# A hybrid diffusion block on one core: gate and up projections by seven products a pair, and the hidden split moved into the down stage

## The chip, the cores and the metric

The kernel runs on one core of a Trainium2 chip. The metric is device microseconds of one execution, the median over several runs. The profiled execution gives the span from its first to its last instruction. Engines are named as in the profile: PE (TensorE), PEld (its weight loads), DVE (VectorE), ACT (ScalarE), POOL (GpSimd), SP (the queue that issues DMAs).

## What is computed

One transformer-like layer over 512 latent tokens of width 1024 (with a context of 256 tokens): a token mixer of three branches (a state-space scan, a convolution, a pooling mixer), merged by gates and projected, and then a dense SwiGLU with a hidden width of 2816:

```python
def swiglu(h, w_gate, w_up, w_down):
    return (jax.nn.silu(h @ w_gate) * (h @ w_up)) @ w_down
...
        h_lat = modulate(rms_norm(x, norm2_g[l]), mod_lat[3], mod_lat[4])
        x = x + mod_lat[5] * swiglu(h_lat, ffn_w_gate[l], ffn_w_up[l], ffn_w_down[l])
...
    return rms_norm(x, final_g)
```

The change touches `swiglu` alone: 512 x 1024 times 1024 x 2816 twice, and 512 x 2816 times 2816 x 1024.

## The kernel before

Tokens lie along the free dimension (512 columns), features along the 128 partitions. Each projection is tiled by 128 output features. A weight tile of a unit is 128 x 1024: eight blocks of 128 x 128, one for each 128 input features. Operands are F32R, and each product is made in three passes: a number is split into a high part, rounded to F32R, and a low part, the rest. `mm3` (lines 131 to 136) adds hi·hi, hi·lo and lo·hi into one PSUM bank, so a unit with eight input tiles is 24 matmuls of 512 columns.

`load_unit` (115 to 125) loads a weight tile from SP into one of three `wr` tiles (line 112), casts it on ACT to `whi` (line 120) and subtracts on DVE to `wlo` (line 122 or 124); `whi` and `wlo` have three tiles each. `split` (127 to 129) does the same to any tile. PSUM has three banks "mm" and four "ps".

Up to line 1064 the token mixer and the residual run; they end with `h2`, the eight normalised input tiles as hi and lo (`hh`, `hl`), made by halves of the tokens (1047 to 1054). Then:

- Lines 1072 to 1080: the first three units, by halves of the tokens (256 columns), so that they can start before the second half of `h2` is there.
- Lines 1083 to 1102: the units u = 3 to 43; an even u is the gate, an odd one the up part of pair u // 2, 22 pairs in all. The gate's bank goes through Silu on ACT (1091), the up bank is multiplied with it on DVE (1093), and the product is split at once into `fh` and `fl` (1095). In eight of the pairs an `ada` step (line 900, DVE) makes a column of the last modulation vector from a 512 KB load of `wada`.
- Lines 1105 to 1122: eight down tiles of 66 matmuls, with three weight units each, the residual, and the final norm; the last tile goes by halves.

Engines run their queues in order. Since line 1016's `load_unit` all this is issued through `nc.vector`, `nc.scalar` and `nc.tensor`, and the tile framework orders each queue by a planner's priorities; `tc.high_priority` moves a step forward. A step waits for what it reads, and for the readers of what its tile held before.

## Time and profile before

| what | value |
|---|---|
| median of 3 runs | 1000.64 us (1000.06 to 1000.73) |
| span of the profiled execution | 998.8 us |
| time of the profiled execution beside it | not listed; the median is 1.8 us above the span |
| PE, DVE, ACT busy | 977.7, 670.9, 411.9 us |
| gate and up units u = 3 to 43 | 641.20 to 866.40 us |
| down tiles | 866.40 to 988.9 us |

A matmul's busy time runs from its start to a modelled end and overlaps the next; the pace of PE is read from starts or from counts in a stretch. A row's "idle before" is the time in which its engine stood still just ahead of it, with what ended it.

### The profile page before, as it was taken

What the parts mean: (1) busy time and instruction counts of PE and PEld (TensorE: products, weight loads), DVE (VectorE), ACT (ScalarE), POOL (GpSimd) and SP (SyncE); (2) the same over time, 40 slices, a digit from 0 to 9 for tenths busy, and PEclk for the clock granted to TensorE, in tenths of its full rate; (3) what the DMA queues carried; (4) which work ended last, traced back from release to release, by engine and by line L of the source; (5) the groups of instructions that cost most, each with busy time, mean ns of one, the idle gap of its engine ahead of it and who ended that gap; (6) DMA issues with size and microseconds to landing.
All of it is one profiled execution on the core that took longest, in us unless ns stands there. A gap on an engine that the chain in (4) does not pass through costs nothing.

```text
span 998.8 us, 12631 instructions
## 1 busy us (share of the span) xinstructions
PE 977.7 (98%) x4820; PEld 789.1 (79%) x4820; DVE 670.9 (67%) x1014; ACT 411.9 (41%) x598; POOL 20.7 (2%) x68
## 2 busy tenths in 40 slices
PE   6999999999999999999999999999999999999996
PEld 4678888888887776676787889988888888888885
DVE  5589999978889999999877846734453333332333
ACT  5683643244454233346655545523223232232331
POOL 0100000000000000001000000000000000000000
PEclk9999999999999999999999999999999999999998
DMA  9653334322122466545689851433443222233312
GB/s 364 264 181 106 121 112 145 107 85 78 43 85 77 135 203 201 188 152 170 193 278 326 320 184 43 149 106 126 148 141 133 91 99 94 85 100 95 96 58 85
DMA packets 59149, 144.04 MB, mean 144 GB/s; under 512 B 11728, under 2 KB 22608, under 8 KB 57936
## 3 DMA queue, kind: packets, MB, share of 16 engines
q1 hardware_dynamic: 59088, 143.23, 43.0%
q8 instruction: 38, 0.62, 0.2%
q14 instruction: 23, 0.19, 0.1%
HBM read 126.44 MB, written 16.78 MB: 143 GB/s over the span
## 4 chain that ended last, share of the span: by engine, by line
PE 89%; DVE 4%; DMA 4%; ACT 1%; issue 1%; SPq 0%; DVEq 0%; ACTq 0%
PE mm L134 26%; PE mm L136 26%; PE mm L135 25%; DMA wr<-in_wso_dram 1%; PE mm L61 1%; PE ps L1077 1%; PE ps L794 1%; DMA wr<-in_wada_dram 1%; PE y L864 1%; PE ps L853 1%; PE ps L61 1%; PE ps L746 1%; DVE A L408 1%; DMA W<-yd 1%; PE ps L831 1%
## 5 line engine op out<-in xcount | busy, mean ns | idle before, releaser
L136 PE MATMUL mm<-hh,wlo 128*128 128x512 f32 x864 | 341.9, 396 | 1.1 <-DVE wlo L122 1.1
L134 PE MATMUL mm<-hh,whi 128*128 128x512 f32 x864 | 342.4, 396 | 0.3 <-ACT whi L120 0.3
L135 PE MATMUL mm<-hl,whi 128*128 128x512 f32 x864 | 341.6, 395 | 0.0
L120 ACT CAST whi<-wr 128x1024 fp32r<-128x1024 f32 (+1 forms) x151 | 155.1, 1029 | 372.5 <-PE mm L135 236.7
L122 DVE TENSOR_TENSOR wlo<-wr,whi 128x1024 fp32r<-128x1024 f32 (+1 forms) x148 | 176.1, 1192 | 143.0 <-ACT whi L120 137.3
L136 PEld LDWEIGHTS mm<-hh,wlo 128*128 128x128 f32 x864 | 162.3, 188 | 41.2 <-issue 4.3
L135 PEld LDWEIGHTS mm<-hl,whi 128*128 128x128 f32 x864 | 162.4, 188 | 38.2 <-issue 4.3
L134 PEld LDWEIGHTS mm<-hh,whi 128*128 128x128 f32 x864 | 162.4, 188 | 37.1 <-issue 3.0
L408 DVE SCALAR_TENSOR_TENSOR A<-U,vec_t,A 128x512 f32<-128x512 f32 x180 | 128.0, 751 | 0.3 <-ACT A L403 0.3
L134 PE MATMUL mm<-fh,whi 128*128 128x512 f32 (+1 forms) x198 | 72.5, 366 | 0.1
L136 PE MATMUL mm<-fh,wlo 128*128 128x512 f32 (+1 forms) x198 | 72.5, 366 | 0.0
L135 PE MATMUL mm<-fl,whi 128*128 128x512 f32 (+1 forms) x198 | 72.5, 366 | 0.0
L700 DVE SCALAR_TENSOR_TENSOR C<-C,vec_t,C 128x772 f32<-128x772 f32 (+1 forms) x48 | 46.9, 977 | 4.7 <-ACT C L698 2.2
L1093 DVE TENSOR_TENSOR tmp<-mm,tmp 128x512 f32<-128x512 f32 x21 | 14.5, 689 | 46.5 <-PE mm L136 46.5
L134 PEld LDWEIGHTS mm<-fh,whi 128*128 128x128 f32 x198 | 37.3, 189 | 6.7 <-DVE X L997 0.5
L135 PEld LDWEIGHTS mm<-fl,whi 128*128 128x128 f32 x198 | 37.3, 189 | 6.1
L136 PEld LDWEIGHTS mm<-fh,wlo 128*128 128x128 f32 x198 | 37.3, 189 | 6.0
L134 PE MATMUL mm<-H,whi 128*128 128x256 f32 (+1 forms) x124 | 37.4, 301 | 0.0
L135 PE MATMUL mm<-H,whi 128*128 128x256 f32 (+1 forms) x124 | 37.2, 300 | 0.0
L136 PE MATMUL mm<-H,wlo 128*128 128x256 f32 (+1 forms) x124 | 37.2, 300 | 0.0
L900 DVE CUSTOM_DVE_ANT_0 wr<-wr,C,vec_t 128x1024 f32<-128x1024 f32 x24 | 30.7, 1279 | 1.8 <-DMA wr<-in_wada_dram 1.7
L900 DVE CUSTOM_DVE_ANT_0 wr<-wr,sil_f,vec_t 128x1024 f32<-128x1024 f32 x8 | 10.3, 1284 | 24.4 <-DMA wr<-in_wada_dram 24.4
(319 smaller groups left out, 1153.9 us busy)
## 6 DMA issues: line engine op xcount, KB each, us to landing
wr<-in_win_dram SPq DMA_DIRECT2D x62, 512.0 KB
wr<-in_wgu_dram SPq DMA_DIRECT2D x44, 512.0 KB
wr<-in_wada_dram SPq DMA_DIRECT2D x32, 512.0 KB
wr<-in_wdn_dram SPq DMA_DIRECT2D x16, 512.0 KB
X<-in_wad_dram SPq DMA_DIRECT2D x4, 1024.0 KB
H<-in_wad_dram SPq DMA_DIRECT2D x4, 1024.0 KB
mrg<-tmp SPq DMA_DIRECT2D x16, 256.0 KB
gat<-tmp SPq DMA_DIRECT2D x16, 256.0 KB
```

The source lines that it names most:

```text
L61: return lambda *a, **k: tc.keep_in_program_order(op(*a, **k))
L120: S.copy(hi[:, :n], raw[:, :n])
L122: V.tensor_tensor(lo[:, :n], raw[:, :n], hi[:, :n], ALU.subtract)
L134: PE.matmul(o, hi[:, col : col + P], rh, start=first, stop=False)
L135: PE.matmul(o, hi[:, col : col + P], rl, start=False, stop=False)
L136: PE.matmul(o, lo[:, col : col + P], rh, start=False, stop=last)
L408: V.scalar_tensor_tensor(accs[e], pads[e](k), vc("dw_w", (2 * j + e) * 31 + k), accs[e], ALU.mult, ALU.add)
L700: tap = V.scalar_tensor_tensor(a[:, 0:n], pad[:, k : n + k], vc("conv_w", i * 5 + k), a[:, 0:n], ALU.mult, ALU.add)
L746: PE.matmul(st[:, d * P : (d + 1) * P], btokc[:, z, i // 4, :], xw[:, d, z, :], start=z == 0, stop=z == 1)
L794: PE.matmul(sp, btok[:, z, g, :], xw, start=True, stop=True)
L900: V.tensor_tensor_reduce(raw, raw, silb[0], 1.0, vc("b_ada", i), ALU.mult, ALU.add, mod_l[:, i : i + 1])
L1093: V.tensor_tensor(sg, o, sg, ALU.mult)
```

## The change

Pairs 0 to 2 and 21 stay as they are, save that their gated product is kept whole in F32 ("hid", 22 tiles). Pairs 3 to 20 take a form of Strassen's product. The weight block of a pair is cut in gate and up, and in two halves of input features; the tokens are cut in a left and a right half. Seven products of a quarter each (four input tiles, three passes, 256 columns: 12 matmuls) take the place of eight. Four of them, p1, p2, p3 and p4 in the code, have a plain operand on one side at least; the others need sums:

- Of the tokens, once: `token_sums` adds hi and lo of `h2` to full tiles, makes four combinations, and splits each into a hi and a lo "T" tile.
- Of the weights, for each pair: `sa` and `sb` hold four combinations of half tiles of `g` and `u`, made on DVE in F32, and split into "shi" and "slo". `g` is split whole, `u` by its second half.
- Of the products: p1, p6, p5 and p3 go to one bank, `b1`, each but the first adding to what is there, and ACT or DVE reads the bank between them; p7 and p4 go to `b2`, p2 to `b3`. `gt` and `ut` collect gate and up.

The products of a pair are woven with those of the pair before: p1, p5 of the last pair, p7, p4 of the last, p6, p3 of the last, p2.

The down stage starts with the 22 splits of "hid", into tiles that the fast pairs used ("shi", "slo", "T", "S", "hh"). The eight `ada` steps move there too, one a down tile.

```diff
--- before.py
+++ after.py
@@ -16,6 +16,8 @@
 KT = 8
 EPS = 1e-6
 NFF = 22
+PLAIN_HEAD = 3
+PLAIN_TAIL = 1
 NW = 8
 NM = 3
 GATES_BEFORE_LN = 5
@@ -1080,29 +1082,165 @@
                 PE.matmul(o[:, sl], lo[:, k * P : (k + 1) * P], h2[k][0][:, sl], start=False, stop=k == KT - 1)
 
     hid = []
-    for u in range(2 * NFF):
+
+    def plain(u):
         if u < 3:
-            o = first[u][1]
-        else:
-            w, o = ffn_unit(u)
-            project(o, [(w, KT)], h2, whole[0])
-        if u % 2 == 0:
-            sg = tmp()
-            S.activation(sg, o, AF.Silu)
-            continue
-        V.tensor_tensor(sg, o, sg, ALU.mult)
-        hi, lo = pt(f2, [P, T], "fh", NFF, F32R), pt(f2, [P, T], "fl", NFF, F32R)
-        split(hi, lo, sg)
-        hid.append((hi, lo))
-        i = u // 2
-        if i == 4:
-            load_sil(f2.tile([P, 1024], F32, tag="sil", name="sil_f"))
-            adas.extend((5, q) for q in range(8))
-        if 6 <= i < 14:
-            ada(1)
+            return first[u][1]
+        w, o = ffn_unit(u)
+        project(o, [(w, KT)], h2, whole[0])
+        return o
+
+    def gated(up, sg):
+        h = pt(f2, [P, T], "hid", NFF)
+        V.tensor_tensor(h, up, sg, ALU.mult)
+        hid.append(h)
+
+    def plain_pair(i):
+        sg = tmp()
+        S.activation(sg, plain(2 * i), AF.Silu)
+        gated(plain(2 * i + 1), sg)
+
+    H = T // 2
+    left, right = slice(0, H), slice(H, T)
+
+    def half_tiles(k0, sl):
+        return [tuple(a[:, sl] for a in h2[k0 + k]) for k in range(4)]
+
+    def quad(tag, bufs, dt=F32):
+        return pt(f2, [P, 4, H], tag, bufs, dt)
+
+    def token_sums():
+        full = []
+        for q in range(4):
+            full.append(pt(f2, [P, 2, T], ("shi", "slo")[q % 2], 4))
+            for e in range(2):
+                V.tensor_tensor(full[q][:, e, :], *h2[2 * q + e], ALU.add)
+        made = []
+
+        def put(dst, fn):
+            for q in range(2):
+                V.tensor_tensor(dst[:, 2 * q : 2 * q + 2, :], *fn(q), ALU.subtract)
+            hi, lo = quad("T", 8, F32R), quad("T", 8, F32R)
+            split(hi, lo, dst)
+            made.append([(hi[:, k, :], lo[:, k, :]) for k in range(4)])
+            return dst
+
+        t3 = put(quad("S", 2), lambda q: (full[q + 2][:, :, right], full[q][:, :, right]))
+        t1 = put(quad("S", 2), lambda q: (full[q][:, :, right], full[q][:, :, left]))
+        t2 = put(quad("S", 2), lambda q: (full[q + 2][:, :, right], t1[:, 2 * q : 2 * q + 2, :]))
+        put(quad("S", 2), lambda q: (full[q + 2][:, :, left], t2[:, 2 * q : 2 * q + 2, :]))
+        return made
+
+    def fast_pair(i):
+        g, u = (load_raw(wgu[i, :, e * 1024 : (e + 1) * 1024], 1024) for e in range(2))
+        c = slice(0, T), slice(T, 2 * T)
+        sa, sb = pt(f2, [P, 2 * T], "S", 2), pt(f2, [P, 2 * T], "S", 2)
+
+        def parts(src, n, tag=None):
+            if tag is None:
+                hi, lo = pt(per, [P, 1024], "whi", 3, F32R), pt(per, [P, 1024], "wlo", 3, F32R)
+            else:
+                hi, lo = pt(f2, [P, 1024], "shi", 4, F32R), pt(f2, [P, 1024], "slo", 4, F32R)
+            split(hi[:, :n], lo[:, :n], src)
+            return hi, lo
+
+        wa = parts(g, 1024)
+        V.tensor_tensor(sa[:, c[0]], g[:, c[0]], u[:, c[0]], ALU.subtract)
+        V.tensor_tensor(sb[:, c[0]], u[:, c[0]], u[:, c[1]], ALU.add)
+        V.tensor_tensor(sa[:, c[1]], sb[:, c[0]], g[:, c[0]], ALU.subtract)
+        ws = parts(sa, 1024, 1)
+        V.tensor_tensor(sb[:, c[1]], g[:, c[1]], sa[:, c[1]], ALU.subtract)
+        wt = parts(sb, 1024, 1)
+        wu = parts(u[:, c[1]], T)
+        b1, b2, b3 = mmp(), psp(), psp()
+        gt, ut = tmp(), tmp()
+
+        def product(o, w, base, rhs, first):
+            for k in range(4):
+                cs = slice(base + k * P, base + (k + 1) * P)
+                for n, (x, y) in enumerate(((w[0], 0), (w[0], 1), (w[1], 0))):
+                    PE.matmul(
+                        o[:, left], x[:, cs], rhs[k][y],
+                        start=first and k + n == 0, stop=k == 3 and n == 2, skip_group_check=True,
+                    )
+
+        def p1():
+            product(b1, wa, 0, x11, True)
+            with tc.high_priority():
+                S.copy(gt[:, left], b1[:, left])
+
+        def p7():
+            product(b2, ws, 0, d3, True)
+            with tc.high_priority():
+                S.copy(ut[:, right], b2[:, left])
+
+        def p6():
+            product(b1, ws, T, d2, False)
+            with tc.high_priority():
+                S.copy(ut[:, left], b1[:, left])
+
+        def p2():
+            product(b3, wa, T, x21, True)
+            with tc.high_priority():
+                V.tensor_tensor(gt[:, left], gt[:, left], b3[:, left], ALU.add)
+                S.activation(gt[:, left], gt[:, left], AF.Silu)
+
+        def p5():
+            product(b1, wt, 0, d1, False)
+            with tc.high_priority():
+                V.tensor_tensor(ut[:, right], ut[:, right], b1[:, left], ALU.add)
+
+        def p4():
+            product(b2, wu, 0, d4, False)
+            with tc.high_priority():
+                V.tensor_tensor(ut[:, left], ut[:, left], b2[:, left], ALU.add)
+
+        def p3():
+            product(b1, wt, T, x22, False)
+            with tc.high_priority():
+                S.activation(gt[:, right], b1[:, left], AF.Silu)
+                gated(ut, gt)
+
+        return (p1, p7, p6, p2), (p5, p4, p3)
+
+    for i in range(2):
+        plain_pair(i)
+    d3, d1, d2, d4 = token_sums()
+    x11, x21, x22 = half_tiles(0, left), half_tiles(4, left), half_tiles(4, right)
+    for i in range(2, PLAIN_HEAD):
+        plain_pair(i)
+    load_sil(f2.tile([P, 1024], F32, tag="sil", name="sil_f"))
+    adas.extend((5, q) for q in range(8))
+    tail = ()
+    for i in range(PLAIN_HEAD, NFF - PLAIN_TAIL):
+        head, nxt = fast_pair(i)
+        for n in range(4):
+            head[n]()
+            if n < len(tail):
+                tail[n]()
+        tail = nxt
+    for f in tail:
+        f()
+    for i in range(NFF - PLAIN_TAIL, NFF):
+        plain_pair(i)
+
+    hs = []
+    for q in range(NFF // 2):
+        tags = ("shi", "slo") if q < 4 else ("T", "T") if q < 8 else ("S", "S") if q < 9 else None
+        if tags:
+            pair = [pt(f2, [P, 2, T], tag, {"T": 8, "S": 2}.get(tag, 4), F32R) for tag in tags]
+        for e in range(2):
+            if tags:
+                hi, lo = (a[:, e, :] for a in pair)
+            else:
+                hi, lo = (pt(per, [P, T], "hh", 8, F32R) for _ in range(2))
+            split(hi, lo, hid[2 * q + e])
+            hs.append((hi, lo))
+    hid = hs
 
     acc = pt(per, [P, T], "sum", 1)
     for m in range(8):
+        ada(1)
         o = mmp()
         ws = [(load_unit(wdn[m, :, k0 * P : (k0 + kn) * P], kn * P), kn) for k0, kn in ((0, 8), (8, 8), (16, 6))]
         for sl in halves if m == 7 else whole:
@@ -1115,7 +1253,7 @@
             rms_tail(ms, sl)
             n = T // 2
             for q in range(4):
-                ot = pt(per, [P, 2, n], "hh", 8)
+                ot = pt(f2, [P, 2, n], "hid", NFF)
                 V.tensor_tensor(
                     ot, x1[:, 2 * q : 2 * q + 2, sl], acc[:, sl].unsqueeze(1).to_broadcast([P, 2, n]), ALU.mult
                 )
@@ -1230,7 +1368,7 @@
     from concourse.bass_utils import run_bass_kernel_spmd
 
     d = _layout(inputs)
-    nc = bacc.Bacc("TRN2", target_bir_lowering=False, num_devices=1)
+    nc = bacc.Bacc("TRN2", target_bir_lowering=False, num_devices=1, dynamic_dma_scratch_size=1024)
     arrays, args = {}, []
     for name in _ORDER:
         a = np.ascontiguousarray(d[name])
```

Three places show what this does to the queues. First DVE, in two plain pairs of before (two units each; `wlo` is a weight's low part, `fl` that of the gated product):

```order
L122 TENSOR_TENSOR wlo_5863<-wr_5860,whi_5862 128x1024
L129 TENSOR_TENSOR fl_5785<-tmp_5750,fh_5784 128x512
L122 TENSOR_TENSOR wlo_5896<-wr_5893,whi_5895 128x1024
L1093 TENSOR_TENSOR tmp_5819<-mm_5827,tmp_5819 128x512
L122 TENSOR_TENSOR wlo_5932<-wr_5929,whi_5931 128x1024
L129 TENSOR_TENSOR fl_5854<-tmp_5819,fh_5853 128x512
```

and in one steady fast pair of the change (`S` are the combinations, L131 a split's low part, L1191, L1196 and L1185 the additions after p5, p4 and p2, L1095 `gated`):

```order
L1148 TENSOR_TENSOR S_6216<-wr_6212,wr_6214 128x512
L1149 TENSOR_TENSOR S_6217<-wr_6214 128x512
L1191 TENSOR_TENSOR tmp_5992<-tmp_5992,mm_5988 128x256
L1150 TENSOR_TENSOR S_6216<-S_6217,wr_6212 128x512
L1152 TENSOR_TENSOR S_6217<-wr_6212,S_6216 128x512
L131 TENSOR_TENSOR slo_6226<-S_6216,shi_6225 128x1024
L1196 TENSOR_TENSOR tmp_5992<-tmp_5992,ps_5989 128x256
L131 TENSOR_TENSOR wlo_6219<-wr_6212,whi_6218 128x1024
L131 TENSOR_TENSOR slo_6231<-S_6217,shi_6230 128x1024
L1095 TENSOR_TENSOR hid_6196<-tmp_5992,tmp_5991 128x512
L1185 TENSOR_TENSOR tmp_6116<-tmp_6116,ps_6115 128x256
L131 TENSOR_TENSOR wlo_6235<-wr_6214,whi_6234 128x512
```

Six steps in two units became twelve in a pair, among them four that read PSUM banks or what comes from them.

Second, the start of pair 3. PE's queue from the end of its p1 (`mm_5779` is its `b1`, `mm_5863` that of pair 4, `ps_5780` and `ps_5781` its `b2` and `b3`):

```order
L1162 MATMUL mm_5779<-hl_5187,whi_5759 128x256
L1162 MATMUL mm_5779<-hh_5186,wlo_5760 128x256
L1162 MATMUL mm_5863<-hh_5180,whi_5843 128x256
L1162 MATMUL mm_5863<-hl_5181,whi_5843 128x256
L1162 MATMUL mm_5863<-hh_5180,wlo_5844 128x256
L1162 MATMUL ps_5780<-T_5659,shi_5766 128x256
L1162 MATMUL ps_5780<-T_5660,shi_5766 128x256
L1162 MATMUL mm_5779<-T_5673,shi_5766 128x256
L1162 MATMUL mm_5779<-T_5674,shi_5766 128x256
L1162 MATMUL ps_5781<-hh_5188,whi_5759 128x256
L1162 MATMUL ps_5781<-hl_5189,whi_5759 128x256
```

and DVE's queue there (`wlo_5844` is the low part of pair 4's `g`, `slo_5767` that of pair 3's `sa`):

```order
L1149 TENSOR_TENSOR S_5758<-wr_5755 128x512
L1095 TENSOR_TENSOR hid_5748<-mm_5723,tmp_5684 128x512
L1150 TENSOR_TENSOR S_5757<-S_5758,wr_5753 128x512
L131 TENSOR_TENSOR wlo_5844<-wr_5837,whi_5843 128x1024
L1152 TENSOR_TENSOR S_5758<-wr_5753,S_5757 128x512
L131 TENSOR_TENSOR slo_5767<-S_5757,shi_5766 128x1024
L131 TENSOR_TENSOR slo_5772<-S_5758,shi_5771 128x1024
L1148 TENSOR_TENSOR S_5841<-wr_5837,wr_5839 128x512
```

Three matmuls of pair 4 stand ahead of pair 3's p7, and the split that they read stands behind most of the work on the token sums.

Third, the end of the fast pairs. ACT's queue (`mm_7863` is pair 20's `b1`, `mm_7738` pair 19's; `shi` and `T` here take splits of "hid"; L1201 is the Silu after p3):

```order
L122 CAST whi_8006<-wr_8004 128x1024
L130 CAST shi_8075<-hid_5748 128x512
L1180 COPY tmp_7867<-mm_7863 128x256
L130 CAST shi_8075<-hid_5946 128x512
L130 CAST T_8099<-hid_6821 128x512
L1201 ACTIVATE tmp_7741<-mm_7738 128x256
L130 CAST shi_8081<-hid_6071 128x512
```

and DVE's (`hid_7946` is pair 19's product, L1191 the addition that reads pair 20's `b1` after p5):

```order
L131 TENSOR_TENSOR slo_8076<-hid_5946,shi_8075 128x512
L1095 TENSOR_TENSOR hid_7946<-tmp_7742,tmp_7741 128x512
L131 TENSOR_TENSOR slo_8082<-hid_6071,shi_8081 128x512
L1185 TENSOR_TENSOR tmp_7866<-tmp_7866,ps_7865 128x256
L131 TENSOR_TENSOR slo_8082<-hid_6196,shi_8081 128x512
L1191 TENSOR_TENSOR tmp_7867<-tmp_7867,mm_7863 128x256
```

The splits of the down stage have moved in between the last steps of the fast pairs, on both engines.

## Rows read from the trace of the kernel before

**Rows 1.** The page: busy us by engine, and the chain that ended last by engine.

```profile
PE 977.7 (98%) x4820; PEld 789.1 (79%) x4820; DVE 670.9 (67%) x1014; ACT 411.9 (41%) x598; POOL 20.7 (2%) x68
...
PE 89%; DVE 4%; DMA 4%; ACT 1%; issue 1%; SPq 0%; DVEq 0%; ACTq 0%
```

**Rows 2.** Four stretches: length; busy us of PE, PEld, DVE, ACT, POOL; clock; DMA.

```profile
180.00:200.00 20.00, 20.00 (x89) 16.33 (x88) 20.00 (x30) 5.26 (x7) 0.17 (x3) 1.00 0.40 114
641.20:866.40 225.20, 225.20 (x986) 184.81 (x985) 87.68 (x100) 65.94 (x84) 0.00 (x0) 1.00 0.35 119
866.40:972.00 105.60, 105.60 (x470) 87.50 (x470) 32.62 (x35) 30.25 (x35) 0.00 (x0) 1.00 0.29 87
974.40:979.40 5.00, 5.00 (x44) 5.00 (x44) 0.00 (x0) 0.00 (x0) 0.00 (x0) 1.00 0.00 0
```

**Rows 3.** Chain of waits, the split first units: start, length, engine, tile, line.

```profile
632.88 5.65 PE ps L1077 x48
638.54 2.83 PE ps L1080 x24
```

**Rows 4.** PE in order of time, first and last matmul of two stretches of 256 columns.

```profile
605.70 0.28 PE L136 MATMUL mm<-H,wlo 128*128 128x256 f32 x1
...
611.46 0.28 PE L136 MATMUL mm<-H,wlo 128*128 128x256 f32 x1
...
974.34 0.28 PE L134 MATMUL mm<-fh,whi 128*128 128x256 f32 x1
...
979.50 0.28 PE L135 MATMUL mm<-fl,whi 128*128 128x256 f32 x1
```

**Rows 5.** Groups by line and shape, 600 to 1000 us: busy us, mean ns of one.

```profile
L134 PEld LDWEIGHTS mm<-fh,whi 128*128 128x128 f32 x198 | 37.3, 189 | 6.7 <-DVE X L997 0.5
...
L129 DVE TENSOR_TENSOR fl<-tmp,fh 128x512 fp32r<-128x512 f32 x22 | 15.1, 686 | 5.6 <-ACT fh L128 5.6
...
L128 ACT CAST fh<-tmp 128x512 fp32r<-128x512 f32 x22 | 13.8, 625 | 18.0 <-DVE tmp L1093 17.9
...
L1052 DVE TENSOR_TENSOR C<-C,sum 128x256 f32<-128x256 f32 x16 | 5.9, 417 | 0.0
...
L997 DVE SCALAR_TENSOR_TENSOR X<-mm,mod_l,A 128x256 f32<-128x256 f32 x6 | 2.9, 483 | 3.7 <-PE mm L136 3.7
...
L140 ACT ACTIVATE tmp<-ps,eps_t 128x256 f32<-128x256 f32 x4 | 1.9, 468 | 0.7 <-PE ps L1002 0.6
```

**Rows 6.** DVE in order of time, at the first gate and up units and at the end.

```profile
635.37 0.88 DVE L1054 SCALAR_TENSOR_TENSOR hl<-C,mod_l,hh 128x256 fp32r<-128x256 f32 x2 [0.24 <-ACT hh L1053]
639.57 3.50 DVE L122 TENSOR_TENSOR wlo<-wr,whi 128x1024 fp32r<-128x1024 f32 x3 [3.32 <-PE ps L1080]
...
984.61 2.50 DVE L1119 TENSOR_TENSOR hh<-X,sum 128x512 f32<-128x512 f32 x4
```

**Rows 7.** ACT in order of time, casts of weights in the first gate and up units.

```profile
638.15 2.95 ACT L120 CAST whi<-wr 128x1024 fp32r<-128x1024 f32 x3 [0.90 <-ACT junk L1064]
...
652.22 1.05 ACT L120 CAST whi<-wr 128x1024 fp32r<-128x1024 f32 x1 [3.92 <-PE mm L135]
```

**Rows 8.** Loads in order of time: issue and use, one as a step of the chain.

```profile
531.82 0.38 SPq L974 DMA_DIRECT2D C<-mrg  x1
...
535.45 6.64 DMA wr<-in_wso_dram
...
536.96 0.46 SPq L112 DMA_DIRECT2D wr<-in_wso_dram  x1
...
698.50 0.33 SPq L112 DMA_DIRECT2D wr<-in_wada_dram  x1
...
701.74 1.29 DVE L900 CUSTOM_DVE_ANT_0 wr<-wr,sil_f,vec_t 128x1024 f32<-128x1024 f32 x1 [3.27 <-DMA wr<-in_wada_dram]
...
731.46 0.33 SPq L112 DMA_DIRECT2D wr<-in_wada_dram  x1
...
735.80 1.28 DVE L900 CUSTOM_DVE_ANT_0 wr<-wr,sil_f,vec_t 128x1024 f32<-128x1024 f32 x1 [4.37 <-DMA wr<-in_wada_dram]
```

## The prediction

> **What bounds the kernel now.** I read the busy table first [rows 1]: TensorE (PE) is busy 98% of the span, VectorE (DVE) 67%, ScalarE (ACT) 41%, and the chain that ended last is 89% PE. [...]
>
> 41 units of 24 matmuls (984) take 225.20 us: **228.9 ns for a 512-column matmul**, 5.49 us a unit, **10.99 us a pair**. That pace doesn't depend on DVE: from 180 to 200 us DVE is busy 20.00 of 20.00, and PE still does its 89 in 20 us [rows 2].
>
> **What a 256-column matmul costs.** The kernel has them in three places. In the split first units 48 take 5.65 and 24 take 2.83 us [rows 3]: 117.8 ns. In the w_out halves the starts 605.70 and 611.46 lie 48 matmuls apart, in the last down tile 974.34 and 979.50 lie 43 apart [rows 4]: 120 ns each. The first place runs all hi passes before the lo passes, the other two the order hi·hi, hi·lo, lo·hi, which `product` has too. I take **120**, and keep 117.8 as the other end. Both are over half of 228.9, so the price of halving is already in them. From 974.40 to 979.40 the weight loads (PEld) are busy 5.00 of 5.00 us, where they were 184.81 of 225.20 with 512 columns [rows 2].
>
> [...]
>
> **The change, part by part.**
>
> *Products.* Eighteen of 22 pairs (3 to 20) issue 84 matmuls of 256 columns instead of 48 of 512: 84 x 0.120 = 10.08 us for 10.99, **0.91 a pair, 16.3 us in all** (19.6 at 117.8). All of it is on PE's path.
>
> *Weight forming.* A pair used to cost DVE two 1024 splits and two 512 operations. Behind one another these take 1.14 (three in 3.50 less the 0.08 by which rows overlap) and 0.605 (four in 2.50) [rows 6]: 3.5 us. Now it is three 1024 splits, four combinations, one 512 split, `gated`, and three 256 additions out of PSUM (no such row: 0.42 to 0.48 by a sum in SBUF and a PSUM operation with two steps [rows 5]; I take 0.4 behind one another): 3.4 + 2.4 + 0.6 + 0.6 + 1.2 = 8.2 of 10.08 us. ACT: three casts of 0.95 (three in 2.95 [rows 7]), a half one of 0.6, three copies and two Silu of 256 at about 0.45 (0.47 where one reads PSUM [rows 5]): 5.7. Both fit. What must fit too is the ring through the three `wr` tiles: the load of `u` of pair n+1 takes the tile of `g` of pair n, free once the split of that `g` ends. Then: load 3.24 (issued 698.50, used 701.74 [rows 8]), three combinations 1.8, cast of `sa` 1.05, its low part 1.14, one addition 0.4, the next split of `g` 1.23: **8.9 us**, under 10.08. The other wait in DVE's queue, on p4 before that split, is PE's own pace. The split ends about 2 us before p1 of the next pair wants it. So I cost weight forming in the steady pairs at nothing; its cover is PE's 10.08, and if it is gone each further us of the ring costs 18.
>
> *Token sums and the start.* 16 operations of 0.605 and four splits of 1.14: 14.2 us of DVE, before pair 3 starts, at 641.20 + 3 x 5.49 = 657.7. After the last `h2` row (ends 636.25) [rows 6] DVE's queue has six sums to 639.9 and three splits to 643.3; `gated`, two sums and four differences to 647.5; `gated` behind unit 3 to 648.2; three splits to 651.6; five operations and two splits to 656.9; two combinations, `gated` behind unit 5, a combination to 659.5; the split of pair 4's `g` to 660.6; then `sb` and the low part of `sa` to 662.4. PE ends p1 of pair 3 at 659.1, and the next in its order is the start of p1 of pair 4, whose third matmul, due at 659.3, wants the split of 660.6: **1.3 us** lost. It and the 14 behind it then last until 662.4. Pair 4's `u` can load only after 661.2, lands at 664.5, and its low part of `sa` is ready at 669.0, where PE comes at 668.2: **0.8**. Together 2.1; from 0, if DVE is quicker, to 5, if a load comes late.
>
> *Down stage.* 22 splits (0.63 on ACT, 0.69 on DVE [rows 5]) and eight `ada` steps move from gate/up into the last pairs and the down stage, where DVE is busy 32.62 of 105.60 us [rows 2]. PE takes a hidden tile each 0.69 us, DVE makes one each 0.605, and most are made before unit 43 ends; the cover is those 11 us of the last plain pair, without it up to 13 us would show. I cost them at nothing, and the eight `wada` loads on SP's queue too (3.24 us each against 15 us a tile). What they do is stand in ACT's queue: the cast into a T tile of pair 20's p5 stands ahead of the Silu of p3 of pair 19, so after p5 come that cast 0.6, Silu 0.45, `gated`, a low part, an addition, a low part, the addition that reads `b1` (0.6 + 0.6 + 0.4 + 0.6 + 0.4) and handovers of about 0.2. Only then may p3 of pair 20 write `b1`: 3.85 us, of which p4 covers 1.44. **2.4 us lost**, from 0 to 5.
>
> *Nothing:* the smaller DMA scratch (all the loads in question stand on SP), the output tiles taken from "hid".
>
> **Sum.** -16.3 + 2.1 + 2.4 = -11.8 us against the profiled execution (span 998.8 to 987.0; it has no other time on the page). The median of the runs, 1000.64, is 1.8 us above that span and I keep this: **988.8 us**.
>
> **Rivals.**
>
> *A, the shorter spacing.* At 117.8 ns the pairs save 19.6 us: 1000.6 - 19.6 + 4.5 = 985.5, without the two stalls 981. For it: one place of three, the one that reads `h2` as the change does; against it: its order of passes isn't the change's.
>
> *B, the ring paces the pair.* One of the `wada` loads took 4.34 (731.46 to 735.80 [rows 8]), which gives a ring of 10.0, just under PE's. Between 4.4 and 5.1 us a load would make the pair 10.1 to 10.7; the middle, 10.4, gives 995.
>
> *C, slower.* The same ring with a load of 6.64 (from 535.45 on the chain [rows 8]): 12.3 us a pair, 18 x 2.2 more than my forecast: 1029. It decides from a landing of 5.1 us on (pair 10.7, the gain eaten by the two stalls). For it: DVE's queue is in order, so a late `u` holds up every drain behind it. Against it: that load is one of eight transfers issued from 531.82 to 536.96 [rows 8], where a fast pair has two loads in 10 us.
>
> *D, weight loads are not hidden.* Here a load takes 188 ns [rows 5] beside matmuls that start each 120. Were it in line, a pair would take 84 x 0.308 = 25.9 us instead of 48 x 0.417 = 20.0, 106 us slower: about 1106. [...]
>
> *E, no effect.* A spacing of 131 ns (48 x 228.9 / 84) would save nothing: 1000 to 1005 with the stalls. No row has it, but T tiles and accumulation over two products in one bank are new.
>
> **Chances.** Forecast 0.56 (its own range 984 to 994, stalls of 0 to 10), A 0.19, B 0.13, C 0.08, D 0.01, E 0.03. 0.2% is 2.0 us, about what these runs can tell from no change. Faster: forecast, A and 0.10 of B, 0.85. Same: 0.02 of B and E, 0.05. Slower: C, D and the rest of B, 0.10. The range goes from A without most of its stalls, 981.5, to the greater part of B, 998; C to E and B's end stay out.
>
> **What the profile will show.** Right: in the steady pairs PE idle near 0, p1 to p1 10.1 us, DVE some 80% busy, its waits on PE. The stalls at the start (PE behind DVE's `wlo`) and at the end (PE behind DVE's L1191) add to 3 to 7 us. Wrong: a pair of 10.5 or more with PE waiting on `wlo` each time and DVE's combination on the load (B, C); PE gapless but at over 125 ns (E); PE waits within the first down tile.

## The result and the profile after

The kernel after takes **984.63 us** (median; 984.43 to 986.65, 4 runs), the kernel before 1000.35 in the same comparison (1000.02 to 1000.73, 4 runs): ratio 0.9844, 95% interval 0.9830 to 0.9858. The profiled span went from 998.8 to 982.9, 15.9 us less. Line numbers of the kernel after are two or more higher; its products stand on one line, 1162.

The page of the kernel after, busy us by engine, against [rows 1]:

```profile
PE 961.0 (98%) x5468; PEld 807.9 (82%) x5468; DVE 781.8 (80%) x1196; ACT 465.6 (47%) x710; POOL 20.7 (2%) x68
```

PE is still the bound (88% of the chain that ended last, 89% before): 648 matmuls more (18 pairs with 36 more each) and 16.7 us less of busy time. DVE took over 110.9 us of work, ACT 53.7.

Three stretches of the kernel after (length; busy us of PE, PEld, DVE, ACT, POOL; clock; DMA), against [rows 2]: gate and up from the first plain unit after the split ones to the first down matmul, a steady pair, the first 21.7 us of the down stage.

```profile
640.39:850.26 209.87, 208.42 (x1634) 202.86 (x1633) 187.95 (x264) 119.52 (x196) 0.00 (x0) 1.00 0.33 110
674.71:684.72 10.01, 10.01 (x87) 10.01 (x86) 9.70 (x14) 5.49 (x10) 0.00 (x0) 1.00 0.35 117
850.26:872.00 21.74, 21.74 (x97) 17.92 (x96) 7.87 (x11) 6.81 (x8) 0.00 (x0) 1.00 0.43 135
```

The granted clock is 1.00 in these stretches, as in those of [rows 2], so no part of the difference is clock. In the kernel before, the same stage starts at 641.20 [rows 2], and its first down matmul at 866.44:

```profile
866.44 0.40 PE L134 MATMUL mm<-fh,whi 128*128 128x512 f32 x1
```

So gate and up took 225.24 us before and 209.87 now, both from start to start: 15.4 of the 15.9 us come from this stage. In the whole of it PE is idle for 1.45 us. A steady pair in the chain of waits (start, length, engine, tile, line), where [rows 3] had the split units:

```profile
674.71 2.86 PE mm L1162 x24
677.57 2.88 PE ps L1162 x24
680.45 2.85 PE mm L1162 x24
683.31 1.41 PE ps L1162 x12
```

The seven products stand here in PE's order: p1 and the last pair's p5 (674.71), p7 and p4 (677.57), p6 and p3 (680.45), p2 (683.31). Eighty-four matmuls take 10.01 us, 119.1 ns each. p1, p3 and p2, which read `hh` and `hl`, take 1.41 to 1.42 us (117.8 to 118.2 ns a matmul), the four that read T tiles 1.44 (120 ns).

The waits of PE and its weight loads in this stage, and DVE's three most frequent (engine, line, waited for: us in total, times, longest), 640.39 to 866:

```profile
DVE slo L131 <- ACT shi L130: 5.9, 27, 0.5
DVE S L1148 <- DMA wr<-in_wgu_dram: 5.8, 10, 1.3
DVE wlo L131 <- ACT whi L130: 5.5, 10, 1.3
...
PE mm L1162 <- DVE wlo L131: 1.3, 1, 1.3
...
PEld mm L1162 <- DVE tmp L1191: 0.2, 1, 0.2
```

PE waits once for 1.3 us, for a low weight part; at the end its weight load waits 0.2 on L1191. The many waits of DVE are short, and none of them reaches PE in a steady pair. From one turn of DVE's queue in such a pair, the rows with a wait:

```profile
741.49 1.23 DVE L131 TENSOR_TENSOR wlo<-wr,whi 128x1024 fp32r<-128x1024 f32 x1 [0.30 <-ACT whi L130]
742.93 1.23 DVE L131 TENSOR_TENSOR slo<-S,shi 128x1024 fp32r<-128x1024 f32 x1 [0.21 <-ACT shi L130]
...
746.20 0.69 DVE L1148 TENSOR_TENSOR S<-wr,wr 128x512 f32<-128x512 f32 x1 [0.17 <-DMA wr<-in_wgu_dram]
...
749.33 1.23 DVE L131 TENSOR_TENSOR slo<-S,shi 128x1024 fp32r<-128x1024 f32 x1 [0.19 <-ACT shi L130]
...
751.50 1.23 DVE L131 TENSOR_TENSOR wlo<-wr,whi 128x1024 fp32r<-128x1024 f32 x1 [0.54 <-ACT whi L130]
```

The split of `g` at 741.49 ends at 742.72, the load that takes its tile has landed by 746.20, and the next split of `g` comes 10.01 us after this one: PE's pace, with 1.1 us of short waits in DVE's queue from the end of the first to the start of the next.

### The profile page after: what moved, and what is told of

The parts are those of the page before. It is cut to its first block, busy times and chain, and to the rows that moved or that the text cites. A ratio compares the mean times of both kernels' runs of the same rounds, so it can differ in the third digit from the quotient of the medians.

```text
span 982.9 us, 14243 instructions
## 1 busy us (share of the span) xinstructions
PE 961.0 (98%) x5468; PEld 807.9 (82%) x5468; DVE 781.8 (80%) x1196; ACT 465.6 (47%) x710; POOL 20.7 (2%) x68
## 4 chain that ended last, share of the span: by engine, by line
PE 88%; DVE 5%; DMA 3%; ACT 1%; issue 1%; SPq 0%; DVEq 0%; ACTq 0%
PE mm L137 19%; PE mm L136 19%; PE mm L138 19%; PE mm L1162 10%; PE ps L1162 8%; PE mm L63 1%; DMA wr<-in_wso_dram 1%; PE ps L1079 1%; PE ps L796 1%; DMA wr<-in_wada_dram 1%; PE y L866 1%; PE ps L855 1%; PE ps L63 1%; PE ps L748 1%; DVE A L410 1%
## 5 line engine op out<-in xcount | busy, mean ns | idle before, releaser
L138 PE MATMUL mm<-hh,wlo 128*128 128x512 f32 (+1 forms) x612 | 242.5, 396 | 0.5 <-DVE wlo L124 0.5
L136 PE MATMUL mm<-hh,whi 128*128 128x512 f32 (+1 forms) x612 | 242.3, 396 | 0.3 <-ACT whi L122 0.3
L137 PE MATMUL mm<-hl,whi 128*128 128x512 f32 x576 | 230.2, 400 | 0.0
L138 PEld LDWEIGHTS mm<-hh,wlo 128*128 128x128 f32 x612 | 115.2, 188 | 28.8 <-issue 4.3
L136 PEld LDWEIGHTS mm<-hh,whi 128*128 128x128 f32 x612 | 115.2, 188 | 27.3 <-issue 3.0
L137 PEld LDWEIGHTS mm<-hl,whi 128*128 128x128 f32 x576 | 108.4, 188 | 26.0 <-issue 4.3
L1162 PE MATMUL mm<-T,shi 128*128 128x256 f32 x288 | 53.5, 283 | 0.0
L131 DVE TENSOR_TENSOR slo<-S,shi 128x1024 fp32r<-128x1024 f32 x36 | 44.1, 1225 | 5.9 <-ACT shi L130 5.9
L1162 PEld LDWEIGHTS mm<-T,shi 128*128 128x128 f32 x288 | 44.9, 191 | 0.0
L130 ACT CAST whi<-wr 128x1024 fp32r<-128x1024 f32 (+1 forms) x36 | 30.1, 836 | 25.9 <-PE ps L1162 21.2
L1162 PE MATMUL mm<-T,slo 128*128 128x256 f32 x144 | 40.9, 284 | 0.0
L131 DVE TENSOR_TENSOR wlo<-wr,whi 128x1024 fp32r<-128x1024 f32 (+1 forms) x36 | 34.5, 958 | 7.1 <-ACT whi L130 5.5
L902 DVE CUSTOM_DVE_ANT_0 wr<-wr,sil_f,vec_t 128x1024 f32<-128x1024 f32 x8 | 10.3, 1283 | 23.6 <-DMA wr<-in_wada_dram 23.6
```

The costliest lines, as they stand in the source:

```text
L130: S.copy(dst_hi, src)
L131: V.tensor_tensor(dst_lo, src, dst_hi, ALU.subtract)
L136: PE.matmul(o, hi[:, col : col + P], rh, start=first, stop=False)
L137: PE.matmul(o, hi[:, col : col + P], rl, start=False, stop=False)
L138: PE.matmul(o, lo[:, col : col + P], rh, start=False, stop=last)
L902: V.tensor_tensor_reduce(raw, raw, silb[0], 1.0, vc("b_ada", i), ALU.mult, ALU.add, mod_l[:, i : i + 1])
```

## The experiments

The theory ahead of the runs: the gain is the shorter matmul time on PE alone; all the new work on DVE and ACT and the ring of loads fit under it; the split of hidden tiles in the down stage costs nothing; the stalls come from the token sums at the start and from the order of DVE's and ACT's queues at the end. The rivals: the move itself gives or takes time; the last plain pair is what makes the move free; the ring or DVE is as good as full.

Two executions of one program differ by a microsecond or two (the change's four runs span 2.2 us), so where an effect is smaller than that, the stages of the traces are compared: from the first plain gate and up unit after the split ones to the first down matmul. Read from PE's starts:

| run | gate and up, from to (us) | length | steady pair | median, ratio to before (95% interval) |
|---|---|---|---|---|
| before | 641.20 to 866.44 | 225.24 | 10.99 | 1000.35 |
| after | 640.39 to 850.26 | 209.87 | 10.01 | 984.63, 0.9844 (0.9830 to 0.9858) |
| e1_plain | 641.10 to 866.34 | 225.24 | 10.99 | 1000.26, 1.0002 (0.9994 to 1.0011) |
| e2_tail0 | 641.24 to 849.77 | 208.53 | 10.01 | 983.91, 0.9833 (0.9820 to 0.9846) |
| e3_head4 | 639.41 to 847.98 | 208.57 | 10.01 | 983.45, 0.9832 (0.9819 to 0.9846) |
| e4_wr2 | 639.28 to 848.56 | 209.28 | 10.01 | 985.20, 0.9845 (0.9831 to 0.9858) |
| e5_wr2_held | 639.74 to 853.91 | 214.17 | 10.0 to 10.7 | 989.86, 0.9897 (0.9883 to 0.9910) |
| e6_order | 640.16 to 849.00 | 208.84 | 10.01 | 983.88, 0.9840 (0.9826 to 0.9853) |
| e7_pad | 641.39 to 849.71 | 208.32 | 9.89 | 984.24, 0.9837 (0.9823 to 0.9850) |
| e8_dve2 | 639.92 to 860.96 | 221.04 | 10.70 | 995.74, 0.9959 (0.9945 to 0.9972) |
| e9_map | 639.59 to 847.33 | 207.74 | 9.87 | 984.33, 0.9842 (0.9826 to 0.9859) |
| e10_combo | 640.57 to 846.33 | 205.76 | 9.89 | 981.57, 0.9813 (0.9799 to 0.9828) |
| e11_combo192 | 641.11 to 847.15 | 206.04 | 9.89 | 978.99, 0.9796 (0.9780 to 0.9811) |
| e12_wshift | 639.73 to 847.03 | 207.30 | 9.83 | 982.14, 0.9824 (0.9811 to 0.9837) |

### The move alone

```diff
-PLAIN_HEAD = 3
-PLAIN_TAIL = 1
+PLAIN_HEAD = 22
+PLAIN_TAIL = 0
...
-    d3, d1, d2, d4 = token_sums()
```

> All 22 pairs are plain (48 matmuls of 512 columns, no token sums, no 7-product pair); the gated product is still split in the down stage and the eight ada steps stand there too. Theory (the whole gain is the products on PE, the move is worth nothing): the time is that of the kernel before, 1000.4 within 1, and PE waits nowhere in the first down tile by more than 0.5 us. Rival 1 (taking the split and the ada steps out of the gate and up stage is what saved time): 985 to 995. Rival 2 (the move itself costs, up to the 13 us named for a down stage without cover): above 1002, with PE waiting on the split hidden tiles.

1000.26 us, ratio 1.0002 (0.9994 to 1.0011). The gate and up stage is as long as in the kernel before (225.24 both times), though 7 us of DVE work left it, and the down stage that took this work over has no wait of PE. Gate and up, and the first down tile, of this kernel:

```profile
641.10:866.34 225.24, 225.24 (x987) 184.80 (x986) 80.67 (x88) 65.50 (x84) 0.00 (x0) 1.00 0.32 104
866.34:882.00 15.66, 15.66 (x70) 12.90 (x69) 6.31 (x8) 4.21 (x5) 0.00 (x0) 1.00 0.31 95
```

PE is busy in all of both. So the move is worth nothing in either direction, and the whole gain of the change belongs to the products. Both rivals fall.

### No plain pair as cover

```diff
-PLAIN_TAIL = 1
+PLAIN_TAIL = 0
```

> PLAIN_TAIL 0: pair 21 is fast too, so no plain pair stands between the last 7-product pair and the down stage. Theory (VectorE and ScalarE split the hidden tiles as fast as PE takes them, so the last plain pair covers little): one pair more at 10.0 instead of 11.0, 983.7, at most 1 us of waits in the first down tile. Rival (the 11 us of the last plain pair are what hides the splits, as the prediction wrote): PE waits for split hidden tiles in the first down tile, several us up to 13, 988 to 997.

983.91 us, beside 984.63 within what such medians tell; the stage is 208.53, 1.3 us shorter. The first down matmul now starts 0.12 us after the last one of the products (849.65 and 849.77), and its first tile shows no wait:

```profile
849.77:865.00 15.23, 15.23 (x69) 12.58 (x68) 12.07 (x18) 6.25 (x12) 0.00 (x0) 1.00 0.50 142
```

DVE is busy 12.07 of 15.23 us here, where the change has 7.87 in 21.74: the splits that the plain pair covered are now made beside the first down tile, and PE waits for none of them. The 11 us of the plain pair were no cover that was needed.

### A later start

```diff
-PLAIN_HEAD = 3
+PLAIN_HEAD = 4
```

> PLAIN_HEAD 4: pair 3 is plain, so the token sums have 11 us more before the first fast pair. Theory (the start stall of 1.26 us is DVE's work on the token sums running late): the stall goes, one gain of 0.98 is lost, 984.3, within 1. Rival (the stall belongs to the ring of load tiles as it starts and not to the sums): the stall of 1.3 stays, 985.6.

983.45 us; the stage took 208.57. The sign of the time is inside the spread, the trace decides: PE is busy 208.57 of 208.57.

```profile
639.41:847.98 208.57, 208.57 (x1599) 201.65 (x1598) 183.98 (x255) 116.91 (x190) 0.00 (x0) 1.00 0.34 111
```

The start stall is gone with 11 us more for the token sums, so it is DVE's work on them, as the first theory said, and not the ring's start. The stall cost more than a pair's gain of 0.98, so one fast pair less is no loss.

### The ring of load tiles

```diff
+    held = pt(per, [P, 1024], "wr", 3)
+    V.memset(held[:, 0:1], 0.0)
     tail = ()
     for i in range(PLAIN_HEAD, NFF - PLAIN_TAIL):
...
     for f in tail:
         f()
+    V.tensor_copy(junk, held[:, 0:1])
```

> One of the three tiles into which gate and up weights are loaded is kept busy during the fast pairs, so that their loads run through two. Nothing else changes. Theory (the ring is load, combinations, splits, release; with three tiles it is a little shorter than PE's 10.0 us): with two tiles a load must wait for the last split of u, the ring holds a load of 3.4 and nearly all of DVE's 9.3 us of a pair, the pair becomes 12.5 to 13.5 and the time 1030 to 1048, PE waiting on the low weight parts in every pair. Rival (loads are far off the path, the ring has room for several us): 984.6 to 990.

985.20 us, nothing changed, and the kernel is why: the planner set the copy that gives the tile back four places behind the memset, before the first fast pair, so three tiles were in use all along. The run tells nothing of the ring. It is the change over again, and a measure of spread: 209.28 for the stage where the change has 209.87, and a span of 981.2 where it has 982.9.

Mended, the read needs the hidden tile of pair 20 and stands behind the fast pairs:

```diff
-    V.tensor_copy(junk, held[:, 0:1])
+    V.tensor_tensor(junk, held[:, 0:1], hid[-1][:, 0:1], ALU.add)
```

> As e4_wr2, but the read that gives the held load tile back now also reads the hidden tile of pair 20, so the tile stays taken until the fast pairs are over and their gate and up loads run through two tiles. (In e4_wr2 the read stood right behind the tile's first write in VectorE's order, so that kernel was the change itself over again.) Theory (the ring of load tiles has about 1 us to spare at three tiles): with two a load waits for the split of u, the ring holds a load of 3.4 and most of DVE's 9 us of a pair: a pair of 12 to 13.5, 1020 to 1048, PE waiting on low weight parts in every pair. Rival (loads are far off the path): 984.6 to 990.

989.86 us, 5.2 more than the change. The theory's 1020 and more is wrong. The number lies at the end of the rival's range, but the rival's reason (loads far off the path) does not hold either. The loads in the chain through two pairs:

```profile
719.54 3.54 DMA wr<-in_wgu_dram
...
740.13 3.60 DMA wr<-in_wgu_dram
```

With two tiles the load does come onto the chain (3.54 and 3.60 us, two pairs apart, 20.59 us from one to the other: 10.3 a pair), but the price is 0.24 us a pair (214.17 against 209.87 over 18), not 2 to 3.5. My sum of the ring took DVE's order of three tiles and put the load behind all of it. The planner ordered the queue anew for two tiles: in every second pair the split of the half `u` tile, which frees a load tile, stands ahead of the two low parts of the combinations instead of behind them. So a ring read off one order says little about another number of tiles. Here the third tile is worth 4 to 5 us (4.3 by the stage), and in the change no wait of a steady pair reaches PE through the ring.

### DVE's room

```diff
         wu = parts(u[:, c[1]], T)
+        for _ in range(2):
+            V.tensor_tensor(wt[1], sb, wt[0], ALU.subtract)
```

> Two more subtractions of 1024 columns on VectorE in every fast pair (the low part of sb made three times over, the result unchanged), 1.14 us each behind one another. Theory (VectorE with its waits has some 1.1 us of slack in a pair of 10.0): a pair becomes about 11.2, 18 pairs cost 18 to 24 us, 1003 to 1009, and DVE is the engine that PE waits on. Rival (the share of DVE's idle time by the page, 20% or 2.0 us a pair, is all usable): at most 0.3 a pair, 984.6 to 990.

995.74 us: 11.1 more than the change, between the two. One pair, its chain from the end of p4 to the next p7, and the first of the two casts with its wait:

```profile
702.81:713.51 10.70, 10.46 (x86) 10.07 (x86) 10.49 (x15) 5.38 (x10) 0.00 (x0) 1.00 0.29 96
```

```profile
710.15 0.49 PE ps L1164 x4
...
710.71 1.05 ACT whi L130
711.76 0.95 ACT shi L130
...
712.76 0.51 PE ps L1164 x2
```

```profile
710.71 1.05 ACT L130 CAST whi<-wr 128x1024 fp32r<-128x1024 f32 x1 [2.44 <-PE ps L1164]
```

The pair is 10.70 us. DVE is busy for 10.49 of them, so with this load no pair could be shorter than that. But DVE is not what p7 waits for: the chain goes from p4 through two casts on ACT. The cast of `whi` waited 2.44 us for p4, and the cast that p7 needs stood behind it, though the combination that it reads was ready at 710.32, and ran at 711.76. For the longer queue of DVE the planner had woven PE's queue anew (the end of p4 now stands right ahead of p3). What part of the 0.69 us more a pair is due to that order and not to DVE is not shown; DVE's own work makes at least 0.48 of it (10.49 - 10.01). Two operations of 1.14 are in the 10.49, so DVE's own work in a pair of the change is 10.49 - 2.28 = **8.2 us**, and less than 1.8 us could be added to it at a pair of 10.01.

### Order of the passes or place of the tiles

```diff
-                for n, (x, y) in enumerate(((w[0], 0), (w[0], 1), (w[1], 0))):
+                for n, (x, y) in enumerate(((w[0], 0), (w[0], 1))):
...
+            for k in range(4):
+                cs = slice(base + k * P, base + (k + 1) * P)
+                PE.matmul(o[:, left], w[1][:, cs], rhs[k][0], start=False, stop=k == 3, skip_group_check=True)
```

> Inside each product the eight hi passes (hi by hi, hi by lo, for the four slices) come first, then the four lo passes, as in the split first units; the count is the same. Theory A (the 117.8 ns belongs to this order of passes, as the prediction took it): all seven products at 1.41 us, pair 9.90, 18 pairs save 1.9 us more: 982.7. Theory B (the spacing goes with the operand tile: 117.8 on hh and hl, 120 on T): products as they are, 1.41 on hh and hl, 1.44 on T, pair 10.0, time 984.6 within 1.

983.88 us. The products on T tiles still take 1.44, those on `hh` and `hl` 1.41, the pair 10.01: the order of passes, by which the prediction had chosen 120 ns, does nothing. Theory B holds.

```diff
             made.append([(hi[:, k, :], lo[:, k, :]) for k in range(4)])
             return dst

+        V.memset(pt(f2, [P, 16], "pad", 1), 0.0)
```

(It stands in `token_sums`, ahead of the first S and T tile; the S tiles, which no matmul of a fast pair reads, move too.)

> A tile of 64 bytes a partition that nobody reads is put ahead of the T tiles, so that they start 64 bytes further on; the matmuls are the same. hh and hl begin at 4672 and 21056 bytes (64 past a multiple of 256), T at 188160 and the weights at 77568 and up (multiples of 256). Theory (where the moving tile lies sets the 2 ns): products on T tiles take 1.41 us like those on hh and hl, pair 9.90, 982.7. Rival (the address means nothing; it is something else about T): 1.44 on T, pair 10.0, 984.6 within 1.

The chain of this kernel, one pair:

```profile
700.90 2.83 PE mm L1163 x24
703.72 1.41 PE ps L1163 x12
705.14 2.83 PE mm L1163 x24
707.96 2.83 PE ps L1163 x24
710.79 2.83 PE mm L1163 x24
```

Every product now takes 1.41 us, the pair 9.89: 64 bytes in the place of a tile are worth 2.2 ns a matmul on it here (120 to 117.8) and 2.0 us over 18 pairs. The theory holds for the pair. The time, 984.24, does not show it: the stage is 1.55 us shorter than the change's, since the wait for the addition out of `b1` near the end grew (0.6 us of PE, where only its weight load had 0.2), and such a difference lies inside the spread of the times. The same tiles read 512 wide in the down stage became slower, 229.6 ns a matmul where they took 226.6 (24 of them in 5.51 and in 5.44 us).

```diff
-            hi, lo = quad("T", 8, F32R), quad("T", 8, F32R)
+            j = len(made)
+            V.memset(pt(f2, [P, (8, 16, 8, 16)[j]], f"pad{j}", 1), 0.0)
+            hi, lo = quad(f"T{j}h", 1, F32R), quad(f"T{j}l", 1, F32R)
```

(The down stage takes the same eight tiles by these names.)

> The change again, but each of the four pairs of T tiles lies at another distance past a multiple of 256 bytes: those of p7 at 32, of p5 at 96, of p6 at 128, of p4 at 192 (in e7_pad all at 64, in the change all at 0). The down stage keeps eight hidden tiles in the same places and reads them 512 columns wide. Theory (the start address modulo 256 sets the 2 ns, and only 64 past it is special, as hh and hl have it): all four products 1.44 us. Rival 1 (only multiples of 256 are slow at 256 columns): all four 1.41, and at 512 columns all four slow, 228.9 ns, where 226.7 is seen on multiples of 256. Rival 2 (it goes by multiples of 64 or 128): 32 and 96 differ from 128 and 192. Time 982.5 to 985 in each case.

984.33 us, and none of the three is right. The first matmul of six products, in PE's order of time (p1, p5, p7, p4, p6, p3):

```profile
712.89 0.28 PE L1164 MATMUL mm<-hh,whi 128*128 128x256 f32 x1
...
714.30 0.28 PE L1164 MATMUL mm<-T1h,shi 128*128 128x256 f32 x1
...
715.73 0.28 PE L1164 MATMUL ps<-T0h,shi 128*128 128x256 f32 x1
...
717.13 0.28 PE L1164 MATMUL ps<-T3h,whi 128*128 128x256 f32 x1
...
718.50 0.28 PE L1164 MATMUL mm<-T2h,shi 128*128 128x256 f32 x1
...
719.93 0.28 PE L1164 MATMUL mm<-hh,shi 128*128 128x256 f32 x1
```

p7 (32 bytes past) takes 1.40, p5 (96) and p6 (128) 1.43, p4 (192) 1.37 us: at four places three lengths, none of them the 1.44 of a multiple of 256. At 512 columns the four places give 233 to 235 ns (24 matmuls in 5.61 us).

```diff
         full = []
+        V.memset(pt(f2, [P, 16], "pada", 1), 0.0)
...
         made = []
+        V.memset(pt(f2, [P, 112], "padb", 1), 0.0)
```

> The change, but its formed weights (shi, slo: operands of p7, p6, p5 and p3) start 64 bytes past a multiple of 256, while T tiles, whi and wlo stay on multiples of 256 and hh and hl 64 past. Theory A (the pace goes by the moving tile's own address): as in the change, 1.44 on T and 1.41 on hh and hl, 984.6. Theory B (it goes by the distance between weights and moving tile): p7, p6 and p5 leave 1.44, and p3, now at distance 0, goes to 1.44; p1, p2 and p4 as they are. Time within 2 of 984.6 in both.

982.14 us, pair 9.83. The first matmul of each product of one pair, with p2 and the next p1 at the end:

```profile
712.74 0.28 PE L1164 MATMUL mm<-hh,whi 128*128 128x256 f32 x1
...
714.10 0.40 PE L1164 MATMUL mm<-T,shi 128*128 128x256 f32 x2
...
715.51 0.40 PE L1164 MATMUL ps<-T,shi 128*128 128x256 f32 x2
...
716.93 0.40 PE L1164 MATMUL ps<-T,whi 128*128 128x256 f32 x2
...
718.36 0.40 PE L1164 MATMUL mm<-T,shi 128*128 128x256 f32 x2
...
719.78 0.28 PE L1164 MATMUL mm<-hh,shi 128*128 128x256 f32 x1
...
721.21 0.28 PE L1164 MATMUL ps<-hh,whi 128*128 128x256 f32 x1
...
722.57 0.28 PE L1164 MATMUL mm<-hh,whi 128*128 128x256 f32 x1
```

p5, p7 and p6, whose weights moved, left 1.44 for 1.41 or 1.42; p3, whose `hh` tiles stayed and whose weights came to the same 64 bytes, went from 1.42 to 1.43; p4, where nothing moved against anything, stays at 1.44 (1.43 in this pair). These five go the way of theory B: the moving tile's own place does not decide alone. But p1 and p2, whose weights and tiles were to stay as they were, went from 1.41 to 1.36, which neither theory has.

The traces have that length elsewhere, where nothing was moved. In e8_dve2, which takes the tiles of the change, eleven matmuls of p2 take 1.25 us in a pair, 113.5 ns each:

```profile
702.64 0.28 PE L1164 MATMUL ps<-hh,whi 128*128 128x256 f32 x1
...
703.89 0.28 PE L1164 MATMUL ps<-T,slo 128*128 128x256 f32 x1
```

And in e7_pad all products from 661.7 to 668.2, p1 among them, go at 113.3 ns, and the same products from 670 on, behind a short gap of PE (668.4 to 668.7), at 117.8:

```profile
665.75 2.38 PE mm L1163 x21
...
671.22 2.83 PE mm L1163 x24
```

So the pace also goes by something other than the tiles' places, and a single length of e9_map or e12_wshift can't be put down to a place with certainty. What is safe is the step from 120 to 117.8 in e7_pad, which all its steady pairs show and none of the change or of e6_order.

### A version that puts it together

`PLAIN_HEAD` 4, `PLAIN_TAIL` 0 and the pad of e7_pad:

> PLAIN_HEAD 4, PLAIN_TAIL 0 and the 64 bytes of e7_pad together: pairs 4 to 21 are fast, T tiles lie as hh and hl do. Theory (the three gains are independent): from the 983.45 of e3_head4 one pair more at 0.98 less, and 18 pairs at 0.11 us less: 980.5, within 1; PE has no wait of over 0.5 us from 640 to the end of the first down tile. Rival (with a pair of 9.9 the ring of load tiles or the down stage without its plain pair shows waits that eat them): 982 to 985.

981.57 us, ratio 0.9813 (0.9799 to 0.9828), an interval just clear of the change's. The stage took 205.76 us, 4.1 less than the change's and 2.8 less than that of e3_head4 (expected 3.0), with PE busy in all of it:

```profile
640.57:846.33 205.76, 205.76 (x1635) 200.69 (x1634) 182.80 (x255) 116.33 (x191) 0.00 (x0) 1.00 0.33 110
```

The median came out 1.1 above the 980.5 expected, inside the spread of 1.7 of its own runs.

```diff
-        V.memset(pt(f2, [P, 16], "pad", 1), 0.0)
...
+            if not made:
+                V.memset(pt(f2, [P, 48], "pad", 1), 0.0)
             hi, lo = quad("T", 8, F32R), quad("T", 8, F32R)
```

> As e10_combo, but the T tiles lie 192 bytes past a multiple of 256 instead of 64, and the S tiles stay on multiples of 256. In e9_map the product whose T tiles lay at 192 (p4) took 1.37 us, where 64 gives 1.41. Theory (the 192 makes it): all four T products at 1.37, pair 9.73, 18 pairs 2.9 us less than e10_combo, and some 0.7 more in the down stage, whose 512-column matmuls on these tiles took 233 ns in e9_map: 979.3, within 1. Rival (p4 is short for its weights or its place in the order): T products 1.41 or 1.44, except p4; 981 to 983.

978.99 us, ratio 0.9796 (0.9780 to 0.9811; 977.97 to 982.48), near the number of the theory and not for its reason: the products on T take 1.41, the pair 9.89 and the stage 206.04, as in e10_combo, and the profiled span is 980.7 where that has 979.3. So 192 bytes do not make 1.37; p4 in e9_map was short for something else. The profiled execution (982.48) is the longest of the five; three of the others took 978 to 979, and no trace shows why. That this version beats e10_combo isn't shown. Both beat the kernel before, and the change (e10_combo by a hair).

## Why the prediction was right, point by point

The forecast was 988.8 (faster); it came to 984.63. In spans, -11.8 was forecast and -15.9 measured. The mechanism was the forecast's own: PE's queue became shorter, nearly everything else stayed under it. The 4.2 us between forecast and result are mostly two terms, the products (1.3) and the stall at the end (2.1 too much); 0.6 come from outside the stage.

**Products.** Forecast -16.3 at 120 ns a matmul; measured 10.99 - 10.01 = 0.98 us a pair, **-17.6**. Mis-sized by 1.3. The step that failed is the choice of 120 for all seven products by the order of passes: three of them go at 117.8 to 118.2 (36 matmuls a pair by some 2 ns are the 1.3 us over 18 pairs), and e6_order shows that the order has no part in it, e7_pad that the tiles' places have. Rival A, 117.8 for all, stands in the same rows as the forecast and was 2.0 off on the other side (-19.6); e7_pad made its pace true.

**Weight forming.** Forecast at nothing, under a DVE load of 8.2 us a pair; e8_dve2 gives 8.2. In the turn shown above the load is used 3.5 us after its tile comes free (742.72 to 746.20), near the 3.24 of [rows 8] and below the 4.34 and 6.64 of rivals B and C, which did not occur. The ring's 8.9 us were right as a verdict. As a model they were poor: two tiles instead of three should have cost 2 us or more a pair by it and cost 0.24.

**The start.** 1.3 us forecast for the wait on `wlo` at the start of pair 4; measured 1.26, at the very matmul named (p1's third, the first low pass):

```profile
658.36 0.28 PE L1162 MATMUL mm<-hl,whi 128*128 128x256 f32 x1
659.89 0.39 PE L1162 MATMUL mm<-hh,wlo 128*128 128x256 f32 x1 [1.26 <-DVE wlo L131]
660.42 0.48 PE L1162 MATMUL ps<-T,shi 128*128 128x256 f32 x2
```

An idle time counts from a modelled end. From start to start the two steps take 1.53 and 0.53 us, where the pace is 0.12, so the wait cost 1.8 us; with the small gaps after it pair 3's start cost 1.9, near the 2.1 forecast. That is luck, since the second stall of the sum, 0.8, did not come: the load on the chain was issued at 657.57, when DVE had ended the second combination of pair 3, and not after 661.2 when the last combination that reads `g` ends. It took the tile of pair 3's `u`, whose readers were done, where the step had it wait for the tile of `g`: three tiles in strict turn, which the planner does not keep to.

**The end.** 2.4 us forecast, 0.3 measured (0.2 before p3's first matmul, 0.1 behind it). ACT's and DVE's queues at that place, in the kernel after:

```profile
833.22 0.62 ACT L130 CAST T<-hid 128x512 fp32r<-128x512 f32 x1
```

```profile
837.28 0.42 DVE L1191 TENSOR_TENSOR tmp<-tmp,mm 128x256 f32<-128x256 f32 x1
```

The cast into a T tile does stand ahead of the Silu of p3, as the step had it, but it ran at 833.22, before p5 of pair 20 had begun (834.66), so it can't have waited for p5's tile. It is the same assumption again, which tile a step gets. From the Silu on the steps follow as listed, the addition at 837.28 releases p3 (837.75), and p4 covers all but 0.2. No row stands behind the handovers of about 0.2 at the end of that list, and no run shows them: the chain here has gaps of 0.01 us ahead of the addition after p2 (836.34) and of 0.04 ahead of p3 (837.70). The mechanism is there: with faster products (e7_pad) PE's wait at this place is 0.6.

**The down stage.** Forecast at nothing, right (e1_plain). Its reason, "the cover is those 11 us of the last plain pair, without it up to 13 us would show", was wrong: without that pair nothing shows (e2_tail0). In the kernel after DVE makes a split in 0.60 us (835.74 to 836.34) where PE takes a hidden tile in 0.69 (three matmuls, 850.26 to 850.96 for the first), so splits made beside the down tile needed no cover at all; the sentence counted all 22 as if PE waited for the last one.

**Together:** -17.6 + 1.9 + 0.3 is -15.4, all that the stage shows. Outside it, the split units ended 0.8 us earlier and the down stage took 0.2 longer, both within what two executions differ by.

**Rival D, weight loads in line.** It did not come true, and the row now says it of this stage: in a steady pair PEld is busy 10.01 of 10.01 us beside a PE that is busy 10.01 as well. A load on L1162 took 187 to 192 ns (medians by tile) beside matmuls that start each 119.1, and the pair took 10.01 us where this rival had 25.9. (The row that the prediction names for a load has 189 ns, not 188; its verdict does not change by it.)

## What to carry to other kernels

Where PE is gapless, count its queue at the pace that the trace shows for that width and those very tiles, and charge the rest only against the engine that would come next: a test load on it (here two operations a pair) tells its own work by how long it is then busy. The longer pair alone does not tell it, since the queues of the other engines may be ordered anew for the load, as they were in e8_dve2. A term that rests on which tile of a pool a step gets is not to be counted without looking at the built order; two of the three stalls forecast fell with that. Work moved into a stage needs no cover as long as it is made there faster than it is used (here a split in 0.60 us, its use in 0.69).

## What the runs showed of the hardware

In these runs the pace of a matmul changed with where its operands lie (120 ns on T tiles in the change, 117.8 in e7_pad, which moves them by 64 bytes), and not with that alone. At 256 columns it went from 113 to 120 ns, at 512 from 226.6 to 235, with shifts of 32 to 192 bytes of a tile and no change of instructions. The two widths don't agree on the better place: T tiles on multiples of 256 bytes took 120 and 226.6, 64 bytes further 117.8 and 229.6. A multiple of 256 doesn't settle it either: in e12_wshift, with T tiles moved by 512 bytes, the down stage's matmuls on them took 228.8 (24 in 5.49 us). By the same run the weights' place seems to count too: p5, p7 and p6, whose weights moved by 64 bytes, took 1.41 or 1.42 us where the change had 1.44. The 113 ns, though, also came and went in one kernel with no tile moved (113.3 and then 117.8 in e7_pad; 113.5 in a p2 of e8_dve2). What sets it, and a rule that covers p4 of e9_map, was not found and stays open.
